# Relative-position softmax: 32 partitions of one late store move to an indirect transfer on GpSimd's queue

## The chip, the cores and the metric

One core of a Trainium2 chip runs the kernel. The metric is the device time of one execution in microseconds (us); less is better. Three executions of the kernel before took 1331.39 to 1331.63 us, median 1331.4.

## What is computed

The reference adds a bias to a stack of 2 x 8 square float32 matrices of S = 2112 rows and columns, and takes a softmax over each row. The bias depends on the head and on the distance of row and column alone, clipped to 16 on either side:

```
rel = pos[:, None] - pos[None, :]
rel_clipped = np.clip(rel, -16, 16) + 16
bias = rel_bias[:, rel_clipped]
logits = logits + bias[None, :, :, :]
logits = logits - logits.max(axis=-1, keepdims=True)
exp = np.exp(logits)
return exp / exp.sum(axis=-1, keepdims=True)
```

Input and output have 285 MB each. Nothing is used twice, so each byte is loaded once and stored once.

## The kernel before

**Tiling.** The 2 x 8 x 2112 rows are dealt to the 128 partitions in blocks: each partition owns 264 rows that follow one another (`ROWS`). The work goes in 44 chunks (`N`), numbered 0 to 43 here; a chunk is six rows (`R`) of every partition, that is 128 pieces of 6 x 2112 x 4 = 50,688 bytes, each in one piece in memory. Four buffers `X0` to `X3` (`NBUF`) hold four chunks; chunk n lies in buffer n mod 4. Chunks 40 to 43 are the last four, and chunk 41, "the last but two", lies in `X1`.

**Staging.** SyncE (SP) issues all loads (line 89) and all stores (line 93) on its queue, q1. VectorE (DVE) adds the bias to a row and takes its negated maximum in one instruction (line 181), ScalarE (ACT) takes the exponential and the row sum (line 190), VectorE takes the reciprocal (line 198) and scales (line 202). All of it works in place in the buffer. The bias comes out of a strip `F` that VectorE copies from `M` in PSUM once for 24 rows (line 175); `M` is built at the start from `rel_bias` and two iotas that GpSimd (POOL) writes (lines 112 and 113).

**What sets the order.** The order is written out by hand; there is no scheduler. `take(engine, semaphore, n)` (line 84) waits until a semaphore has n and takes n off it again. VectorE raises `scaled` once per scaled row. SyncE's stream is:

- six loads of one row each and three of a chunk, for chunks 0 to 3 (lines 98 to 103);
- the store of five rows of chunk 0 (line 219), and its sixth row in 17 transfers (lines 221 to 232), the "fan". The list `FAN` (lines 42 to 47) splits the partitions into nine lanes of every ninth partition, and each lane into two transfers, of k and of the remaining partitions; sorted, they have 15, 14, 13, 12, 11, 10, 9, 8, 7, 7, 6, 5, 4, 3, 2, 1 and 1 rows;
- a loop over chunks (lines 233 to 237): wait for six scaled rows of chunk n, store it, wait until the store of chunk n - 1 has landed (semaphore `st` of its buffer), load chunk n + 3 into that buffer;
- behind the loop, the stores of chunks 41 and 42 (line 239) and the two halves of chunk 43 (lines 240 and 241), which raise `landed`; then waits for the stores still under way (line 243), and for `landed` (line 244).

Load 43 is the last load. It is issued before store 41 and stands ahead of it in the queue.

**GpSimd** writes the two iotas, and at lines 114 to 117 waits for the store of line 219 and the fan, and raises `st[0]` in place of the store of chunk 0. Then it has nothing to do until the end.

Of the kernel before, what the change touches and what calls it, by code (L numbers as in the profile page):

```python
# [8 lines left out]
I32 = mybir.dt.int32  # L9
EXP = mybir.ActivationFunctionType.Exp  # L10
ALU = mybir.AluOpType
# [4 lines left out]
def kernel(  # L16
# [6 lines left out]
    nc = tc.nc  # L23
    P = 128
    B, H, S, S2 = logits.shape
# [3 lines left out]
    ROWS = B * H * S // P  # L29
    PB = S // ROWS  # L30
    assert ROWS * P == B * H * S and PB * ROWS == S and PB == H == 8
    R = 6
    NBUF = 4
    STEP = R * NBUF
    N = ROWS // R
# [2 lines left out]
    MW = S + ROWS - 1  # L38
    FW = S + STEP - 1
    BIG = 3.0e38  # L40
    LANES = 9
    FAN = []
    for lane in range(LANES):
        m = len(range(lane, P, LANES))
        k = 15 if lane == 0 else 15 - lane
# [4 lines left out]
    io = ctx.enter_context(tc.tile_pool(name="io", bufs=1))  # L50
    X = [io.tile([P, R * S], FP32, tag=f"X{b}", name=f"X{b}") for b in range(NBUF)]
# [2 lines left out]
    nmax = io.tile([P, STEP], FP32, tag="nmax", name="nmax")  # L54
    tot = io.tile([P, STEP], FP32, tag="tot", name="tot")
    rec = io.tile([P, STEP], FP32, tag="rec", name="rec")
    ip = io.tile([P, 3, PB], I32, tag="ip", name="ip")
    ps = ctx.enter_context(tc.tile_pool(name="ps", bufs=1, space=bass.MemoryType.PSUM))
    M = ps.tile([P, 4096], FP32, tag="M", name="M")

    def view(t, offset, dims):

        return bass.AP(tensor=t.tensor, offset=t.offset + offset, ap=[[list(t.ap[0])[0], P]] + dims)

    def rows(t, j, n):

        return bass.AP(tensor=t.tensor, offset=t.offset + j * S, ap=[[ROWS * S, P], [1, n * S]])

    with tc.tile_critical(no_gpsimd_drain=True):
        ld = [nc.alloc_semaphore(f"ld{b}") for b in range(NBUF)]  # L70
        st = [nc.alloc_semaphore(f"st{b}") for b in range(NBUF)]
        added = nc.alloc_semaphore("added")
        expd = nc.alloc_semaphore("expd")
        scaled = nc.alloc_semaphore("scaled")
# [2 lines left out]
        pre = nc.alloc_semaphore("pre")  # L77
        idx = nc.alloc_semaphore("idx")
        dve = nc.alloc_semaphore("dve")
        main = nc.alloc_semaphore("main")  # L80
        fan = [nc.alloc_semaphore(f"fan{i}") for i in range(2)]
        landed = tc.alloc_semaphore("landed")

        def take(eng, sem, n):
            eng.wait_ge(sem, n).then_inc(sem, -n)  # L85


        def load(j, b):
            nc.sync.dma_start(out=X[b][:, :], in_=rows(logits, j, R)).then_inc(ld[b], 16)

        def store(j, b, s0=0, n=R, sem=None):
            take(nc.sync, scaled, n)
            nc.sync.dma_start(
                out=rows(out, j + s0, n), in_=X[b][:, s0 * S : (s0 + n) * S]
            ).then_inc(sem or st[b], 16)


        for r in range(R):
            nc.sync.dma_start(
                out=X[0][:, r * S : (r + 1) * S], in_=rows(logits, r, 1)  # L100
            ).then_inc(ld[0] if r == R - 1 else pre, 16)
        for n in range(1, NBUF):
# [6 lines left out]
            out=rbB,  # L109
            in_=bass.AP(tensor=rel_bias.tensor, offset=rel_bias.offset, ap=[[0, P], [1, H * W]]),  # L110
        ).then_inc(rb, 16)
        nc.gpsimd.iota(ip[:, 0], pattern=[[0, PB]], base=0, channel_multiplier=1).then_inc(idx, 1)
        nc.gpsimd.iota(ip[:, 2], pattern=[[1, PB]], base=0, channel_multiplier=0).then_inc(idx, 1)  # L113
        take(nc.gpsimd, main, 16)
        take(nc.gpsimd, fan[0], 16 * ((len(FAN) + 1) // 2))
        take(nc.gpsimd, fan[1], 16 * (len(FAN) // 2))
        nc.gpsimd.sem_inc(st[0], 16)

        v = nc.vector
        done = [0]  # L120
# [21 lines left out]
        for m, op in ((eq, ALU.is_equal), (gt, ALU.is_gt), (le, ALU.is_le), (lt, ALU.is_lt)):  # L142
# [4 lines left out]
            out=view(F, 0, [[W, H], [1, W]]), in0=view(F, 0, [[W, H], [1, W]]),  # L147
# [3 lines left out]
                             axis=mybir.AxisListType.X, op=ALU.add))  # L151
# [5 lines left out]
            out=view(F, 0, [[W, PB], [1, W]]), in0=view(F, SC + 2 * PB, [[1, PB], [0, W]]),  # L157
# [7 lines left out]
            out=view(M, U, [[ROWS, PB], [1, W]]), in0=view(F, 0, [[W, PB], [1, W]]),  # L165
            in1=view(F, SC + 8 * PB, [[1, PB], [0, W]]), op=ALU.add))
        then(v.tensor_copy(out=view(M, U + W, [[ROWS, PB], [1, ROWS - W]]),  # L167
                           in_=view(F, SC + 7 * PB, [[1, PB], [0, ROWS - W]])))
# [8 lines left out]
        def add(b):  # L177
            take(v, ld[b], 16)
            for r in range(b * R, (b + 1) * R):
                x = X[b][:, (r - b * R) * S : (r - b * R + 1) * S]  # L180
                v.tensor_tensor_reduce(  # L181
                    out=x, in0=x, in1=F[:, STEP - 1 - r : STEP - 1 - r + S], scale=-1.0, scalar=BIG,
                    op0=ALU.add, op1=ALU.min, accum_out=nmax[:, r : r + 1],
# [37 lines left out]
        for i, (k, g, lane) in enumerate(FAN):  # L221
            p = g * LANES + lane
            nc.sync.dma_start(
                out=bass.AP(
                    tensor=out.tensor, offset=out.offset + (p * ROWS + R - 1) * S,
                    ap=[[LANES * ROWS * S, k], [1, S]],
                ),
                in_=bass.AP(
                    tensor=X[0].tensor, offset=X[0].offset + p * PSX + (R - 1) * S,
                    ap=[[LANES * PSX, k], [1, S]],  # L230
                ),
            ).then_inc(fan[i % 2], 16)
        with nc.Fori(0, ROWS - 2 * STEP + 1, STEP, engines=[ENG.SP]) as j:
            for b in range(NBUF):
                store(j + (b + 1) * R, (b + 1) % NBUF)
                take(nc.sync, st[b], 16)
                load(j + (b + NBUF) * R, b)
        for n in range(N - NBUF + 1, N - 1):
            store(n * R, n % NBUF)
        store((N - 1) * R, (N - 1) % NBUF, 0, HALF, landed)  # L240
        store((N - 1) * R, (N - 1) % NBUF, HALF, R - HALF, landed)
        for b in range(NBUF - 1):
            take(nc.sync, st[(N + b) % NBUF], 16)
    nc.sync.wait_ge(landed, nc.sync.to_reg(32), synchronizes=[nc.sync.lower_ap(out)])


# [28 lines left out]
```

## Time and profile before

| What | us |
|---|---|
| median of three executions | 1331.4 |
| the profiled execution | 1331.3 |
| span of that execution, from its first to its last instruction | 1329.5 |
| VectorE busy | 976.7 |
| ScalarE busy | 575.2 |
| GpSimd busy | 0.4 |
| share of the span on queue q1, as a share of 16 DMA engines | 99.5% |
| DMA rate over the span | 430 GB/s |

The profile is one execution. Its times are microseconds from the first instruction; `L93` is line 93 of the kernel. `SPq` is the part of SyncE that issues DMAs. A "DMA issue" row gives the size of a transfer and the time from its issue to its landing. A row for a window gives the busy time of each engine in that stretch, then the granted clock of TensorE (not used here), the mean busy share of the 16 DMA engines, and GB/s. A transfer counts in the window in which it starts, so short windows can read over 1.

### The profile page before, as it was taken

Reading aid. Unit: us, or ns where it says so; the run is one execution under the profiler, and the core shown is the slowest. Engines: PE = TensorE matmul, PEld = TensorE weight load, DVE = VectorE, ACT = ScalarE, POOL = GpSimd, SP = SyncE. Lnnn points to the kernel's source line nnn. Section 1 sums busy time; section 2 is a strip of 40 time slices with the busy share of each in tenths; the row PEclk is TensorE's granted clock in tenths of the full one; section 3 lists DMA queues with packets and bytes.
Section 4 is the critical chain, followed back from the end, with each engine's and each line's share of the span. In section 5 each row is a group of like instructions: output and inputs, shape, how many; then the busy total and the mean of one; then the engine's idle time right before and its main releaser. Section 6 shows DMA issues by size and latency. Waiting matters only on the chain. (4 is left out here: it accounts for less than half of the span.)

```text
span 1329.5 us, 2477 instructions
## 1 busy us (share of the span) xinstructions
DVE 976.7 (73%) x911; ACT 575.2 (43%) x539; POOL 0.4 (0%) x6
## 2 busy tenths in 40 slices
DVE  5998767777877776787778767677877776687772
ACT  2565333444444343345444333444444343345440
POOL 0000000000000000000000000000000000000000
DMA  9999999999999999999999999999999999999997
GB/s 391 427 426 424 436 430 433 438 433 435 432 435 435 433 436 430 436 433 435 430 433 439 433 433 427 439 435 432 433 432 438 430 433 430 436 430 436 438 432 337
DMA packets 13939, 571.12 MB, mean 430 GB/s; under 512 B 1648, under 2 KB 1776, under 8 KB 1776
## 3 DMA queue, kind: packets, MB, share of 16 engines
q1 hardware_dynamic: 13792, 570.96, 99.5%
q10 hardware_dynamic: 144, 0.14, 0.1%
q14 instruction: 3, 0.02, 0.0%
HBM read 285.61 MB, written 285.47 MB: 430 GB/s over the span
## 5 line engine op out<-in xcount | busy, mean ns | idle before, releaser
L181 DVE CUSTOM_DVE_ANT_0 X<-X,F 128x2112 f32<-128x2112 f32 x264 | 605.2, 2354 | 302.0 <-DVEq L85 302.0
L190 ACT ACTIVATE X<-X,nmax 128x2112 f32<-128x2112 f32 x264 | 541.7, 2052 | 538.2 <-ACTq L85 516.4
L202 DVE TENSOR_SCALAR X<-X,rec 128x2112 f32<-128x2112 f32 x264 | 332.5, 1316 | 13.2
L190 ACT ACT_TABLE_LOAD x11 | 14.1, 1283 | 185.8 <-ACTq L85 185.8
L190 ACT ACTIVATION_READ_ACCUMULATOR X<-X,nmax 128x1 f32 x264 | 49.2, 186 | 0.0
L175 DVE COPY F<-M 128x2135 f32 x11 | 26.1, 2375 | 6.6 <-DVEq L85 6.6
L181 DVE DVE_READ_ACCUMULATOR2_ANT nmax<- 128x1 f32 x264 | 21.7, 82 | 0.0
L198 DVE RECIPROCAL rec<-tot 128x3 f32<-128x3 f32 x88 | 15.0, 170 | 0.0
L146 DVE TENSOR_TENSOR F<-F 128x264 f32<-128x264 f32 x1 | 0.4, 435 | 4.9 <-DMA F<-in_rel_bias_dram 4.9
L167 DVE COPY M<-F 128x1848 f32<-128x1848 f32 x1 | 2.1, 2077 | 0.0
L133 DVE TENSOR_SCALAR ip<-ip 128x8 int32<-128x8 int32 x1 | 0.2, 172 | 1.3 <-POOL ip L113 1.3
L150 DVE TENSOR_REDUCE rbS<-F 128x33 f32<-128x264 f32 x1 | 0.6, 610 | 0.0
L164 DVE TENSOR_TENSOR M<-F 128x264 f32<-128x264 f32 x1 | 0.4, 441 | 0.0
L156 DVE TENSOR_TENSOR F<-F,rbS 128x264 f32<-128x264 f32 x1 | 0.4, 426 | 0.0
L143 DVE TENSOR_SCALAR F<-F 128x8 f32<-128x8 f32 x4 | 0.4, 167 | 0.0
L169 DVE COPY M<-rbS 128x247 f32<-128x247 f32 x1 | 0.4, 406 | 0.0
L154 DVE TENSOR_SCALAR F<-F,rbS 128x8 f32<-128x8 f32 x1 | 0.2, 231 | 0.0
L160 DVE SCALAR_TENSOR_TENSOR F<-F,rbS 128x8 f32<-128x8 f32 x1 | 0.2, 227 | 0.0
L155 DVE TENSOR_SCALAR F<-F,rbS 128x8 f32<-128x8 f32 x1 | 0.2, 225 | 0.0
L161 DVE SCALAR_TENSOR_TENSOR F<-F,rbS 128x8 f32<-128x8 f32 x1 | 0.2, 221 | 0.0
L136 DVE TENSOR_TENSOR F<-ip 128x8 f32<-128x8 int32 x1 | 0.2, 167 | 0.0
L139 DVE TENSOR_TENSOR F<-ip 128x8 f32<-128x8 int32 x1 | 0.2, 167 | 0.0
(9 smaller groups left out, 1.2 us busy)
## 6 DMA issues: line engine op xcount, KB each, us to landing
X<-in_logits_dram SPq DMA_DIRECT2D x43, 6336.0 KB, 44.7
out_dram<-X SPq DMA_DIRECT2D x42, 6336.0 KB, 52.8
X<-in_logits_dram SPq DMA_DIRECT2D x6, 1056.0 KB, 12.6
out_dram<-X SPq DMA_DIRECT2D x2, 3168.0 KB, 21.9
out_dram<-X SPq DMA_DIRECT2D x1, 5280.0 KB, 34.9
F<-in_rel_bias_dram ACTq DMA_DIRECT2D x1, 132.0 KB, 6.4
out_dram<-X SPq DMA_DIRECT2D x1, 123.8 KB
out_dram<-X SPq DMA_DIRECT2D x1, 115.5 KB
```

The source lines that it names most:

```text
L143: then(v.tensor_scalar(out=m, in0=dp, scalar1=0.0, scalar2=None, op0=op))
L146: then(v.tensor_tensor(out=view(F, 0, [[W, H], [1, W]]), in0=view(F, 0, [[W, H], [1, W]]), in1=view(F, SC + 3 * PB, [[1, H], [0, W]]), op= ...
L150: then(v.tensor_reduce(out=rbS[:, :], in_=view(F, 0, [[1, W], [W, H]]), axis=mybir.AxisListType.X, op=ALU.add))
L156: then(v.tensor_tensor(out=view(F, 0, [[W, PB], [1, W]]), in0=view(F, SC + 2 * PB, [[1, PB], [0, W]]), in1=view(rbS, W - 1, [[0, PB], [-1, ...
L164: then(v.tensor_tensor(out=view(M, U, [[ROWS, PB], [1, W]]), in0=view(F, 0, [[W, PB], [1, W]]), in1=view(F, SC + 8 * PB, [[1, PB], [0, W]] ...
L167: then(v.tensor_copy(out=view(M, U + W, [[ROWS, PB], [1, ROWS - W]]), in_=view(F, SC + 7 * PB, [[1, PB], [0, ROWS - W]])))
L169: then(v.tensor_copy(out=M[:, 0:U], in_=low.to_broadcast([P, U])))
L175: v.tensor_copy(out=F[:, :], in_=M[:, bass.ds(ROWS - STEP - j, FW)]).then_inc(dve, 1)
L181: v.tensor_tensor_reduce(out=x, in0=x, in1=F[:, STEP - 1 - r : STEP - 1 - r + S], scale=-1.0, scalar=BIG, op0=ALU.add, op1=ALU.min, accum_ ...
L190: nc.scalar.activation(out=x, in_=x, func=EXP, scale=-1.0, bias=nmax[:, r : r + 1], accum_out=tot[:, r : r + 1],).then_inc(expd, 1)
L198: v.reciprocal(out=rec[:, r0 : r0 + HALF], in_=tot[:, r0 : r0 + HALF]).then_inc(inv, 1)
L202: v.tensor_scalar_mul(out=x, in0=x, scalar1=rec[:, r : r + 1]).then_inc(scaled, 1)
```

## The change

The store of chunk 41 is split by partition. SyncE stores partitions 0 to 95 as before, with one transfer of 96 pieces. Partitions 96 to 127 (`OWN` to `P`) are stored by GpSimd with indirect transfers: the output is seen as 5632 blocks of 12,672 numbers, one per partition and chunk, and a column of the new tile `sel` has, for each source partition of a transfer, the number of the block that it goes to. `PLAN` lists the transfers as (partitions n, first partition p0, range a to b of the partitions really stored). Partitions outside a to b get a block number past the end (`FAR`), and the transfer skips such pieces (`bounds_check`, `oob_is_err=False`). There are two entries: (112, 0, 0, 0) names partitions 0 to 111 and skips all; (48, 80, 96, 128) names 80 to 127, skips the first 16 and stores the other 32.

GpSimd makes the two columns at the start, an iota and two selects each. After its old waits it waits for `ready`, which SyncE raises once it has seen the six scaled rows of chunk 41, and issues the two transfers. At the end SyncE waits for both (`soft`) beside `landed`. The computation is the same.

```diff
+    OWN = 96
+    PLAN = [(112, 0, 0, 0), (48, 80, OWN, P)]
+    FAR = 1 << 20
+    sel = io.tile([P, len(PLAN)], I32, tag="sel", name="sel")
...
+        for w, (n, p0, a, b) in enumerate(PLAN):
+            col = sel[:, w : w + 1]
+            step(g.iota(col, pattern=[[0, 1]], base=p0 * N + N - 3, channel_multiplier=N))
+            for base, mul in ((p0 - a, 1), (b - 1 - p0, -1)):
+                g.wait_ge(pool, made[0])
+                step(g.affine_select(out=col, in_=col, pattern=[[0, 1]], base=base, channel_multiplier=mul,
+                                     compare_op=ALU.is_ge, fill=float(FAR)))
+        take(g, pool, made[0])
...
+        take(g, ready, 1)
+        blocks = out.rearrange("b h s t -> (b h s t)").rearrange("(n c) -> n c", c=R * S)
+        late = X[(N - 3) % NBUF]
+        lap = list(late.ap[0])[0]
+        for w, (n, p0, a, b) in enumerate(PLAN):
+            g.indirect_dma_start(
+                out=blocks, out_offset=bass.IndirectOffsetOnAxis(ap=sel[0:n, w : w + 1], axis=0),
+                in_=bass.AP(tensor=late.tensor, offset=late.offset + p0 * lap, ap=[[lap, n], [1, R * S]]),
+                in_offset=None, bounds_check=P * N - 1, oob_is_err=False,
+            ).then_inc(soft, 16)
...
-        for n in range(N - NBUF + 1, N - 1):
-            store(n * R, n % NBUF)
+        take(nc.sync, scaled, R)
+        nc.sync.sem_inc(ready, 1)
+        nc.sync.dma_start(
+            out=bass.AP(
+                tensor=out.tensor, offset=out.offset + (N - 3) * R * S, ap=[[ROWS * S, OWN], [1, R * S]]
+            ),
+            in_=X[(N - 3) % NBUF][0:OWN, :],
+        ).then_inc(st[(N - 3) % NBUF], 16)
+        store((N - 2) * R, (N - 2) % NBUF)
...
+    nc.sync.wait_ge(soft, nc.sync.to_reg(16 * len(PLAN)), synchronizes=[nc.sync.lower_ap(out)])
```

More of the change, by code (lines that the diff above doesn't have):

```diff
@@ L40 @@
     BIG = 3.0e38
+    OWN = 96
+    PLAN = [(112, 0, 0, 0), (48, 80, OWN, P)]
+    FAR = 1 << 20
+    assert sorted(p for n, p0, a, b in PLAN for p in range(a, b)) == list(range(OWN, P))
     LANES = 9
@@ L79 @@
         dve = nc.alloc_semaphore("dve")
+        ready = nc.alloc_semaphore("ready")
+        pool = nc.alloc_semaphore("pool")
+        soft = tc.alloc_semaphore("soft")
         main = nc.alloc_semaphore("main")
@@ L113, with step @@
         nc.gpsimd.iota(ip[:, 2], pattern=[[1, PB]], base=0, channel_multiplier=0).then_inc(idx, 1)
+        g = nc.gpsimd
+        made = [0]
+        def step(ins):
+            made[0] += 1
+            ins.then_inc(pool, 1)
+        for w, (n, p0, a, b) in enumerate(PLAN):
[6 more added lines that the diff above has]
+        take(g, pool, made[0])
         take(nc.gpsimd, main, 16)
```

## The prediction

> **What bounds the kernel now.** I read the page first: its totals, then the DMA lines.
>
> ```profile
> span 1329.5 us, 2477 instructions
> DVE 976.7 (73%) x911; ACT 575.2 (43%) x539; POOL 0.4 (0%) x6
> DMA  9999999999999999999999999999999999999997
> DMA packets 13939, 571.12 MB, mean 430 GB/s; under 512 B 1648, under 2 KB 1776, under 8 KB 1776
> q1 hardware_dynamic: 13792, 570.96, 99.5%
> ```
>
> No compute engine is full; the 16 DMA engines are, in 39 slices of 40, and nearly all their work is one queue, q1, SyncE's. 430 GB/s over 16 engines is 26.9 GB/s each, so one row of a chunk (50,688 bytes) costs an engine 1.89 us, a whole chunk (128 rows, 8 per engine) 15.1 us, and one single row of S (8,448 bytes) 0.31 us. The mean of 430 holds short idle at both ends, so these prices are high by a per cent or so. The chain of waits ends in the last scale on VectorE, at 1304.9 us, and says nothing of the 24 us behind it; SyncE's own waits do (the row below it):
>
> ```profile
> 1302.33 2.54 DVE X L202 x2
> ...
> SPq L244 <- DMA out_dram<-X: 14.6, 1, 14.6
> ```
>
> The last thing waited for is the landing of the last store. Now the end of the schedule, from SyncE's timeline and the DMA issues of short windows (load 43, then the stores of chunks 41, 42, and the two halves of 43):
>
> ```profile
> X<-in_logits_dram SPq DMA_DIRECT2D x1, 6336.0 KB, 44.8
> ...
> 1244.93 60.38 SPq L93 DMA_DIRECT2D out_dram<-X  x4
> ...
> out_dram<-X SPq DMA_DIRECT2D x1, 6336.0 KB, 53.0
> ...
> out_dram<-X SPq DMA_DIRECT2D x1, 6336.0 KB, 38.6
> ...
> out_dram<-X SPq DMA_DIRECT2D x1, 3168.0 KB, 20.1
> ...
> out_dram<-X SPq DMA_DIRECT2D x1, 3168.0 KB, 23.6
> ```
>
> and when the four were issued and when load 43 was:
>
> ```profile
> 1238.15 0.35 SPq L89 DMA_DIRECT2D X<-in_logits_dram  x1
> ...
> 1274.95 30.36 SPq L93 DMA_DIRECT2D out_dram<-X  x3
> ...
> 1300.97 0.33 SPq L93 DMA_DIRECT2D out_dram<-X  x1
> ...
> 1304.97 0.33 SPq L93 DMA_DIRECT2D out_dram<-X  x1
> ```
>
> Load 43 lands at 1282.95, store 41 at 1297.9, store 42 at 1313.55, the halves of 43 at 1321.1 and 1328.6. The spaces of 15 and twice 7.5 us are the price of a chunk and of a half: on the engine that lands last, every transfer starts as the one before it ends, and its time is rows times 1.89 us. The other engines are seen in the tail, microsecond by microsecond (third figure from the right: granted clock; then DMA share, GB/s):
>
> ```profile
> 1320.00:1321.00 1.00, 0.00 (x0) 0.00 (x0) 0.00 (x0) 1.00 0.77 329
> 1321.00:1322.00 1.00, 0.00 (x0) 0.00 (x0) 0.00 (x0) 1.00 0.59 253
> 1322.00:1323.00 1.00, 0.00 (x0) 0.00 (x0) 0.00 (x0) 1.00 0.41 177
> 1323.00:1324.00 1.00, 0.00 (x0) 0.00 (x0) 0.00 (x0) 1.00 0.41 177
> 1324.00:1325.00 1.00, 0.00 (x0) 0.00 (x0) 0.00 (x0) 1.00 0.24 101
> 1325.00:1326.00 1.00, 0.00 (x0) 0.00 (x0) 0.00 (x0) 1.00 0.18 76
> 1326.00:1327.00 1.00, 0.00 (x0) 0.00 (x0) 0.00 (x0) 1.00 0.06 25
> 1327.00:1328.00 1.00, 0.00 (x0) 0.00 (x0) 0.00 (x0) 1.00 0.06 25
> ```
>
> A share of 0.06 is one engine of 16. About nine are done by 1322 to 1323, seven still run until 1324, four into 1325, and one alone ends near 1328.1. The shares from 1320 on sum to 2.7 us, so equal loads would end all engines near 1322.7: **5.4 us (0.4%) is the most that moving rows between engines can bring.** Why unequal? In the first chunk, line 223 stores one row per partition by 17 transfers of 15, 14, 13 ... 1, 1 rows. If a transfer of k rows takes the same first k engines, the first engine gets 17 such rows and the last none: 17 times 0.31 is a skew of 5.3 us, near the 7 us seen. Then the six engines with 11 to 17 rows are late by the code, and the tail's seven are these six and one more.
>
> **The change part by part.** The program order on each engine is from the two listings; only POOL, and SyncE at the store of chunk 41, differ.
>
> Start: POOL gets two more iotas and four selects. The nearest rows are its iotas, and the tail of the run gives POOL's and SyncE's small instructions:
>
> ```profile
> 1.04 0.13 POOL L112 IOTA ip<- 128x8 int32 x1 [0.59 <-PEq L270]
> 1.13 0.14 POOL L113 IOTA ip<- 128x8 int32 x1
> ...
> L270 SPq EVENT_SEMAPHORE  x2: 17/17/17, 1329.0 to 1329.5; - x2
> L270 POOLq EVENT_SEMAPHORE_RANGE_CLEAR  x1: 71/71/71, 1329.2 to 1329.2; - x1
> ```
>
> Six times 0.14 is 0.8 us at 1.3 us; they come behind the two iotas that VectorE waits for, and are wanted at 1245. Nothing, unless they took a thousand times as long.
>
> SyncE: the wait for six scaled rows is the old one; the semaphore raise is 0.02 us; the store of 96 rows is issued like that of 128 (0.34). Behind it stand the issues at 1274.95 and later: 30 us of cover. At the end SyncE also waits for the two indirect transfers, begun 80 us before: nothing.
>
> POOL's new wait for that raise has nothing behind it but the two indirect issues and the closing barrier. No row shows an indirect issue; the nearest are 0.33 us for SyncE's. Bounded by zero and ten times that for each: the rows enter the DMA engines between 1246 and 1252. They go by another queue, so they need not stand behind load 43 as store 41 does; they are taken in among load 42, store 40 and load 43. POOL's program has one more instruction behind the last barrier: 0.1 us, on the path (range 0 to 0.5).
>
> DMA work: store 41 gives each engine six rows in place of eight: minus two rows, 3.77 us, on all. The 32 rows come back somewhere. No view shows an indirect transfer, so their division is bounded by cases: even (two each, nothing changes) and in blocks. In blocks, 48 rows over 16 engines are three consecutive ones each; the 16 skipped ones are those of engines 0 to 4 and one of engine 5, so 0 to 4 get none, 5 gets two, 6 to 15 three. I take **blocks**: only they give a meaning to a window of 48 whose first 16 are skipped; for an even spread 32 rows would do. The sum by engine then is minus 3.77 us on 0 to 4, nothing on 5, plus 1.89 on 6 to 15.
>
> [...]
>
> Applied to the tail: the last engine, at 1328.1, is one of the loaded ones and goes to 1324.4; engine 5 stays somewhere between 1324 and 1326; the nine early ones go from at most 1322.5 to 1324.4. The seventh late engine is not among the first six, so it gets one row more: from the near edge of the three that end in 1324 to 1325, 1324.1, to **1326.0. It ends the kernel**, 2.1 us sooner than now. The far edges: it is not late in other runs (minus 3.7 us), or it ends now at 1326.2 (then 1328.1, no gain).
>
> What must not slip: the rows taken in ahead delay load 43 on the engines that get three, by 5.66 us. The seventh engine is 4.0 us ahead of the last, so load 43 lands some 1.7 us later, and so do the scales and the last two issues: 1302.7 and 1306.7. Data follow an issue by about 1.4 us (loads issued at 0.96 us; the DMA share is 0.01 until 2 us and 0.76 from 2 to 4):
>
> ```profile
> 0.96 3.27 SPq L99 DMA_DIRECT2D X<-in_logits_dram  x6
> ...
> 0.00:2.00 2.00, 0.63 (x5) 0.00 (x0) 0.42 (x6) 1.00 0.01 3
> 2.00:4.00 2.00, 0.43 (x5) 0.00 (x0) 0.00 (x0) 1.00 0.76 158
> ```
>
> So the first half is ready at 1304.1. The earliest engine reaches it at 1320.9 less two halves, 1305.8 (now), 1307.7 with its extra row; a relieved one at 1324.6 less 15.1 less 3.77, 1305.7. Covered by 1.6 us; were load 43 late by the whole 5.66 us, the relieved engines would stand idle for 2.3 us. Chunk 42 has more cover, VectorE idle before its next add:
>
> ```profile
> 1283.08 2.36 DVE L181 CUSTOM_DVE_ANT_0 X<-X,F 128x2112 f32<-128x2112 f32 x1 [8.22 <-DVEq L85]
> ```
>
> Sum: the profiled execution took 1331.3 us (span 1329.5 and 1.8 around it), the median is 1331.4. Minus 2.1, plus 0.1, from the median: **1329.4 us.** Its own range is 1327.7 (3.7 gained) to 1331.5 (nothing).
>
> **The rivals.** (1) *The 96 rows take as long as 128.* If the rate of a store depends on which partitions it reads, the lower engines stay at eight row times, the relief is lost and the upper ones still get three rows. Middle engines that end at 1322.4 then end at 1328.1, the seventh at up to 1329.8: 1331.4 to 1333.1. Against it: 17 unequal transfers of line 223 leave no hole in the DMA share; nothing else in the trace has fewer than 128 partitions. [...]
>
> (2) *Even spread.* Two rows each: the ends stay, load 43 is 3.77 us late on the last engine, the first half is ready at 1306.2, 0.4 us late for early engines alone. 1331.5. It would also be the result if the change did not do what its window says.
>
> (3) *Skipped rows are not free*, the slower one. 112 and 16 skipped rows are eight per engine. If each takes time on its engine as a moved row does, that is 15.1 us more on every engine, between 1246 and 1270, and load 43 and all behind it end later: 1344.5. A cost of nothing is what the word skip says; no row decides. It outweighs the gain of 2.1 us from 0.26 us per row, and passes 0.2% from 0.6 us (8 times 0.6 less 2.1 is 2.7); at a third of a row's price it gives 1334.4.
>
> **How the numbers follow.** Two tenths of a per cent, 2.7 us, is about what a measurement of this kernel can tell from no change: 1328.7 and 1334.1. Blocks with free skips: 0.55, of which 0.30 below 1328.7 (the seventh engine's lag may differ in the runs that are timed, and the last engine alone would give 3.7) and 0.25 within. Rival 1: 0.13, of it 0.10 within and 0.03 slower. Rival 2: 0.10, 0.07 and 0.03 (if it meets rival 1 the lower engines carry 3.77 us more, 1335.2). Rival 3: 0.15, slower. 0.07 for what an indirect transfer costs beyond all this, slower. Faster 0.30, same 0.42, slower 0.28. The range goes from 1327.7 to 1335.2, the end of rival 2 with 1; above it lie most of rival 3 and of the rest.
>
> **What would show it.** In the tail of the DMA share after the change: blocks right, if it falls from near 1 to nothing within some 3 us in place of 7, about 1323 to 1326; rival 1, if the share dips between 1283 and 1298, in store 41; rival 2, if the tail is as now; rival 3, if the packets or bytes of GpSimd's queue count more than 32 rows (1.62 MB), or load 43's add starts 10 us late. The step on load 43 is right if that add starts at 1284 to 1286. I am wrong at the root if the last engine now is not one of those with many rows in the first chunk.

## The result and the profile after

The kernel after takes 1335.53 us, the median of eight executions (1334.43 to 1338.07), the kernel before 1331.43 (1331.31 to 1331.72). The ratio is 1.0032, 95% interval 1.0021 to 1.0043: **4.1 us slower**, where 2.0 us faster was forecast. The profiled execution took 1335.25 us. Its page first:

```profile
span 1333.5 us, 2498 instructions
DMA packets 14099, 571.12 MB, mean 428 GB/s; under 512 B 1808, under 2 KB 1936, under 8 KB 1936
q1 hardware_dynamic: 13760, 569.33, 99.2%
q0 software_dynamic: 192, 1.62, 0.3%
```

The bytes are those of before. 1.62 MB, 32 rows, went to GpSimd's queue q0, and 160 packets of hardly any bytes with them: one for each of the 128 skipped rows, and 16 more for each of the two transfers (with one transfer of 48 rows, in no112, q0 has 64 packets). Queue q1 is as full as it was, and yet the span is 4.0 us longer. SyncE's last transfers, from the DMA issues of short windows (KB, then us from issue to landing; load 43 and the stores of chunks 41, 42 and the halves of 43):

```profile
X<-in_logits_dram SPq DMA_DIRECT2D x1, 6336.0 KB, 46.7
...
out_dram<-X SPq DMA_DIRECT2D x1, 4752.0 KB, 57.0
...
out_dram<-X SPq DMA_DIRECT2D x1, 6336.0 KB, 42.0
...
out_dram<-X SPq DMA_DIRECT2D x1, 3168.0 KB, 20.7
...
out_dram<-X SPq DMA_DIRECT2D x1, 3168.0 KB, 24.8
```

With the issues at 1238.45, 1245.32, 1275.29, 1303.18 and 1307.57 they land at 1285.15, 1302.3, 1317.3, 1323.9 and 1332.4. Load 43 is 2.2 us later than before; then store 41, a quarter smaller than it was, lands 4.4 us later than it did, and the transfers behind it land 2.8 to 3.8 us later. VectorE's add of chunk 43 shows the first part, the wait in brackets:

```profile
1285.29 2.36 DVE L214 CUSTOM_DVE_ANT_0 X<-X,F 128x2112 f32<-128x2112 f32 x1 [10.12 <-DVEq L93]
```

The second part is in the windows in which store 41 runs (DMA share, then GB/s, last). The kernel before:

```profile
1285.00:1290.00 5.00, 5.00 (x7) 4.30 (x4) 0.00 (x0) 1.00 0.96 416
1290.00:1295.00 5.00, 5.00 (x6) 4.61 (x5) 0.00 (x0) 1.00 1.05 456
1295.00:1300.00 5.00, 4.85 (x6) 3.98 (x4) 0.00 (x0) 1.00 1.01 436
```

The kernel after:

```profile
1285.00:1290.00 5.00, 4.71 (x5) 2.15 (x2) 0.00 (x0) 1.00 1.02 355
1290.00:1295.00 5.00, 5.00 (x5) 4.68 (x5) 0.00 (x0) 1.00 0.99 314
1295.00:1300.00 5.00, 4.85 (x6) 4.74 (x5) 0.00 (x0) 1.00 0.97 355
```

This pair is the finding. The engines are as busy as before, but move less: the share is near 1 and the rate falls by 15, 31 and 19%. The "busy" engines with a falling rate are here engines whose packets take longer, not engines with more to do: of the rows begun between 1276 and 1304 the slowest took 4.31 us, where before none took more than 1.90. The missing 284 GB/s (1308 less 1024) over 5 us are 1.42 MB, or 3.3 us of all 16 engines at 430 GB/s. The tail then has the old shape, later:

```profile
1322.00:1323.00 1.00, 0.00 (x0) 0.00 (x0) 0.00 (x0) 1.00 0.94 406
1323.00:1324.00 1.00, 0.00 (x0) 0.00 (x0) 0.00 (x0) 1.00 0.82 355
...
1325.00:1326.00 1.00, 0.00 (x0) 0.00 (x0) 0.00 (x0) 1.00 0.59 253
...
1328.00:1329.00 1.00, 0.00 (x0) 0.00 (x0) 0.00 (x0) 1.00 0.29 127
...
1331.00:1332.00 1.00, 0.00 (x0) 0.00 (x0) 0.00 (x0) 1.00 0.06 25
```

The shares of the twelve microseconds from 1320 to 1332 sum to 6.5 us, so equal loads would end near 1326.5, 3.8 us later than before, and the last engine still ends some 5.5 us behind that mean. Not even the spread of the ends was narrowed.

Two more sources are used below, which no view shows. The trace's packet records have the start, the length and the size of each packet, but name no engine. Chained by their ends (in the kernels before and after, all but some 70 of 14,000 packets start within 12 ns of the end of another) they fall into 16 sequences, each taken here as one engine; figures from that are marked *chained*, and where several engines run in step two sequences can be swapped. The trace also has 16 *landing events* for each whole transfer, taken here as one for each engine; they need no chaining.

### The profile page after: what moved, and what is told of

The parts are those of the page before. It is cut to its first block, busy times and chain, and to the rows that moved or that the text cites. A ratio compares the mean times of both kernels' runs of the same rounds, so it can differ in the third digit from the quotient of the medians.

```text
span 1333.5 us, 2498 instructions
## 1 busy us (share of the span) xinstructions
DVE 976.7 (73%) x911; ACT 575.2 (43%) x539; POOL 3.3 (0%) x14
## 3 DMA queue, kind: packets, MB, share of 16 engines
q0 software_dynamic: 192, 1.62, 0.3%
## 5 line engine op out<-in xcount | busy, mean ns | idle before, releaser
L223 ACT ACT_TABLE_LOAD x11 | 14.1, 1283 | 185.8 <-ACTq L93 185.8
```

Of the source, the lines that this page charges most:

```text
L223: nc.scalar.activation(out=x, in_=x, func=EXP, scale=-1.0, bias=nmax[:, r : r + 1], accum_out=tot[:, r : r + 1],).then_inc(expd, 1)
```

## The experiments

Two theories stood against each other. **R**: the rate of a store depends on which partitions its engines read at the same time, and falls with 96 of the 128; such a fall is called a crowd below. **E**: the number of rows on each engine is all that counts, and the loss comes from the indirect transfer; in experiment 5, where that had fallen, E is that a store of fewer than 128 partitions is slow as such. Beside them stood the skipped rows, and the question where a gain could be had.

**1. The machinery without moved rows (skip).** Both indirect transfers are issued with all rows skipped; SyncE stores all 128.

```diff
-    OWN = 96
-    PLAN = [(112, 0, 0, 0), (48, 80, OWN, P)]
+    OWN = P
+    PLAN = [(112, 0, 0, 0), (48, 80, 0, 0)]
```

> The changed kernel with both indirect transfers skipping all their rows, and the store of chunk 41 whole, 128 partitions, on SyncE's queue: the machinery alone. Theories R and E: 1331.4 to 1331.8, no dip in the rate. Theory S (skipped rows or the software queue cost the engines time): some of the 4.1 us, 1332.5 to 1336.

```profile
q0 software_dynamic: 192, 0.00, 0.0%
```

1331.52 us (1331.27 to 1331.89), ratio 1.0001 (0.9992 to 1.0011): no change. 160 skipped rows, two issues, the columns, the raise and the added wait cost nothing that can be measured. In the kernel after the issues have these rows in GpSimd's timeline, 1.07 and 0.88 us, three times SyncE's 0.33:

```profile
1246.25 1.07 POOL L146 DMA_INDIRECT out_dram<-X,sel  x1 [1243.44 <-POOLq L93]
1247.63 0.88 POOL L146 DMA_INDIRECT out_dram<-X,sel  x1 [0.30 <-issue]
```

**2. The store of 96 rows alone (low96).** The kernel before, with store 41 cut to partitions 0 to 95; the other 32 rows are left out, and GpSimd does nothing.

```diff
-        for n in range(N - NBUF + 1, N - 1):
-            store(n * R, n % NBUF)
+        take(nc.sync, scaled, R)
+        nc.sync.dma_start(... ap=[[ROWS * S, 96], [1, R * S]] ..., in_=X[(N - 3) % NBUF][0:96, :])
+        store((N - 2) * R, (N - 2) % NBUF)
```

> The kernel before, with the store of chunk 41 cut to partitions 0 to 95 on SyncE's queue; the other 32 partitions of that chunk are left out of the output, and GpSimd does nothing new. Theory R (the rate of a store falls where its rows lie on few partitions): the DMA rate dips between 1283 and 1300 to about 315 to 355 GB/s at a full busy share, as in the changed kernel, although no indirect transfer runs; the two engine-rows saved are mostly eaten, and the time is 1329.5 to 1333. Theory E (only the number of rows per engine counts): no dip, every engine ends 3.77 us sooner, 1327.6.

1337.76 us (1337.67 to 1337.87), ratio 1.0047 (1.0030 to 1.0064): **1.6 MB less is moved, and it takes 6.3 us more.** Its windows:

```profile
1280.00:1285.00 5.00, 2.06 (x1) 0.00 (x0) 0.00 (x0) 1.00 1.10 365
1285.00:1290.00 5.00, 5.00 (x7) 4.30 (x5) 0.00 (x0) 1.00 1.07 365
1290.00:1295.00 5.00, 5.00 (x5) 4.74 (x5) 0.00 (x0) 1.00 0.85 264
1295.00:1300.00 5.00, 4.85 (x6) 3.85 (x4) 0.00 (x0) 1.00 0.96 375
```

The dip is there without any indirect transfer. E is out. R held as to the dip, but the time that it gave, 1329.5 to 1333, was too low. By the landing events, five engines land store 41 11.2 us behind load 43, six times 1.87. The other eleven, 1.3 to 6.1 us behind these five at load 43, are 3.5 to 16.7 us behind them at store 41.

The cut store alone is also 2.2 us slower than the kernel after, which moves 1.6 MB more. The price is not a fixed one: in sum, the rows begun between 1276 and 1304 take 72 us longer than 1.87 us each here and 55 us in the kernel after (0.1 in the kernel before).

**3. The same bytes from all partitions (thin128).** Store 41 takes the first three quarters of each of the 128 pieces; the rest is left out. The diff is against low96.

```diff
-                ap=[[ROWS * S, 96], [1, R * S]],
-            in_=X[(N - 3) % NBUF][0:96, :],
+                ap=[[ROWS * S, 128], [1, R * S * 3 // 4]],
+            in_=X[(N - 3) % NBUF][0:128, 0 : R * S * 3 // 4],
```

> The kernel before, with chunk 41 stored from all 128 partitions on SyncE's queue but only the first three quarters of each partition's 50,688 bytes: as many bytes as in low96, and the last quarter is left out of the output. Theory R (which partitions a store reads decides): no dip in the DMA rate; all engines end 3.7 us sooner, 1327.7, which is 10 us below low96. Theory B (a store of fewer bytes, or the landing of chunk 41 sooner, is what disturbs the end): a dip as in low96, 1333 or more.

1327.75 us (1327.48 to 1328.07), ratio 0.9972 (0.9962 to 0.9983), and no dip in the same windows:

```profile
1285.00:1290.00 5.00, 5.00 (x7) 4.27 (x4) 0.00 (x0) 1.00 1.00 433
1290.00:1295.00 5.00, 5.00 (x7) 4.60 (x6) 0.00 (x0) 1.00 1.09 471
```

This is the relief of 3.77 us that the prediction counted on. It exists, 10.0 us below low96 for the same bytes; so it isn't the smaller store, or its earlier landing, that disturbs the end.

**4. The upper 96 (up96), and the lower 96 to other places in memory (cross96).** up96 stores partitions 32 to 127 and leaves 0 to 31 out; cross96 reads partitions 0 to 95 and writes them where 32 to 127 belong.

```diff
 up96:    offset ... (32 * ROWS + (N - 3) * R) * S, in_=X[(N - 3) % NBUF][32:128, :]
 cross96: offset ... (32 * ROWS + (N - 3) * R) * S, in_=X[(N - 3) % NBUF][0:96, 0 : R * S]
```

> As low96, but partitions 32 to 127 of chunk 41 are stored and 0 to 31 left out. Theory R: the partitions that crowd are now the upper 64, whose rows are moved by the engines that are early; the late, lowest-numbered engines carry the lower partitions and save their two rows. A dip in the rate as in low96, but a time of 1327.6 to 1330, and 1.5 us or more below low96. Theory E: the same as low96, 1327.6, no dip.

> As low96, from partitions 0 to 95 on chip, but written to the places in memory that belong to partitions 32 to 127; the output is then wrong for chunk 41 (the lowest 32 partitions' places stay empty). Theory R with the source on chip as its cause: as low96, 1337 to 1338.5. Theory H (the places in memory crowd): as up96, 1328.9 to 1330.4.

cross96 takes 1337.78 us (1337.16 to 1338.25), the same as low96: the places in memory don't matter, the source on the chip does. up96 takes 1329.59 (1328.93 to 1330.35), ratio 0.9985 (0.9975 to 0.9995). Its dip is nearly that of low96:

```profile
1285.00:1290.00 5.00, 5.00 (x5) 4.21 (x4) 0.00 (x0) 1.00 1.14 355
1290.00:1295.00 5.00, 5.00 (x7) 4.61 (x6) 0.00 (x0) 1.00 0.90 304
```

In sum its rows take 63 us longer than 1.87 us each, where those of low96 take 72 and those of cross96 74. So most of the 8 us between the two is not in the total but in who pays. Chained: in low96 the engine that is last anyway stretches its six rows by 10.7 us and ends at 1334.7, from 1328.1 less 3.8; in up96 it has no stretch there, and those that stretch by 7 us were early ones.

**5. Half the rows, packed or spread (low64, comb64).** Store 41 has 64 rows, of partitions 0 to 63, or of every second partition; the other 64 are left out. Four rows for each engine in both.

```diff
 low64:  ap=[[ROWS * S, 64], [1, R * S]],      in_: partitions 0 to 63
 comb64: ap=[[2 * ROWS * S, 64], [1, R * S]],  in_: ap=[[2 * PSX, 64], [1, R * S]]
```

> Store 41 has the 64 rows of partitions 0 to 63; the other 64 are left out and nothing goes by GpSimd. The same number of rows on each engine, and the same bytes, as in the store of every second partition run beside it. R: the rate falls to some 300 GB/s or less while store 41 runs and the engines stretch; the four rows take nearly as long as eight and the next store is held up too: 1329 to 1336. E: 1323.9, as the other.

> Store 41 has 64 rows, of every second partition (0, 2, ... 126); the other 64 are left out and nothing goes by GpSimd. Each engine gets four rows in place of eight, and they lie on all of the chip's partitions. R (the partitions read at the same time set the rate, not the number of rows): no dip of the rate, all engines 7.5 us sooner, 1331.4 - 7.5 = 1323.9, with up to 1.5 us lost if engines reach the halves of chunk 43 before they are ready: 1323.5 to 1325.5. E (a store of fewer than 128 partitions is slow as such): as slow as the store of 64 low partitions run beside it.

comb64: 1324.19 us (1323.95 to 1324.28), as forecast. low64: 1327.17 (1326.28 to 1328.65), below the range given, but 3.0 us above comb64. Windows of low64, then of comb64:

```profile
1280.00:1285.00 5.00, 1.21 (x1) 0.00 (x0) 0.00 (x0) 1.00 1.02 264
1285.00:1290.00 5.00, 5.00 (x5) 3.59 (x3) 0.00 (x0) 1.00 0.93 233
```

```profile
1285.00:1290.00 5.00, 5.00 (x5) 3.86 (x3) 0.00 (x0) 1.00 0.98 426
...
1295.00:1300.00 5.00, 4.85 (x7) 4.29 (x4) 0.00 (x0) 1.00 0.73 314
```

With partitions 0 to 63 the rate at a full share falls to 250 to 260 GB/s, under two thirds; with every second partition it doesn't fall. (comb64's 314 at 1295 is the other kind of low rate: the share is low too, 0.73, and 0.63 from 1300 to 1305; the first half of chunk 43 is issued in 1301 to 1303, the second in 1304 to 1308, and from 1305 the share is 1.13.) The number of rows in a store isn't the cause; which partitions they are read from is. low64 came out lower than forecast since the crowd costs less than a halved rate: chained, an engine's four rows and what follows them are stretched by 2.9 to 6.3 us, not by 7.5.

Put to a full share, the windows of low96 (experiment 2) give 332, 341 and 311 GB/s (365 over a share of 1.10, 365 over 1.07 and 264 over 0.85), and there the landing events have five engines unslowed and eleven slowed; those of low64 give 259 and 250, with neighbouring transfers in the windows. Why these partitions slow each other, no run here shows.

**6. Without the skipped 112 (no112), and with it twice (twoskip).** The same 32 rows are moved; only the wholly skipped transfer ahead of them changes.

```diff
 no112:   PLAN = [(48, 80, OWN, P)]
 twoskip: PLAN = [(112, 0, 0, 0), (112, 0, 0, 0), (48, 80, OWN, P)]
```

> The changed kernel without the wholly skipped transfer of 112; its 32 rows go by the transfer of 48 alone. Theories R and E: the rows enter the engines some 13 us sooner, at about 1250 in place of 1265; the time stays at 1334.4 to 1338. Theory S: below 1333.5.

> The kernel after with the wholly skipped transfer of 112 rows issued twice. If each skipped row takes one turn between two rows of SyncE's queue (14 turns of 1.87 us on each engine), the 32 real rows enter some 13 us later, at 1278 to 1290, behind load 43 and among the rows of store 41; the add of chunk 43 on VectorE then starts at 1282.5 to 1283.5 in place of 1285.3. The time: the collision in store 41 stays, and 32 more rows of other partitions are read beside it: 1334 to 1338. If a skipped row is only dropped at once: the same as after in all, the add at 1285.3.

Queue q0 (packets, MB, share) in the windows 1246 to 1262 and 1262 to 1280, of the kernel after:

```profile
q0 software_dynamic: 101, 0.00, 0.4%
...
q0 software_dynamic: 91, 1.62, 21.0%
```

In the first 16 us only packets without bytes go, and all 32 rows follow behind 1262. Without the 112, the same two windows:

```profile
q0 software_dynamic: 50, 1.47, 30.5%
...
q0 software_dynamic: 14, 0.15, 2.4%
```

With the 112 twice, 1262 to 1280 and 1280 to 1296:

```profile
q0 software_dynamic: 173, 0.56, 10.5%
...
q0 software_dynamic: 43, 1.06, 18.4%
```

So a skipped row costs its engine next to no time (each of these packets takes 9 ns in the kernel after; skip has a ratio of 1.0001), but takes a turn: the engine goes back to SyncE's queue for a row after each. Chained, in 140 of the 176 steps from one packet of q0 to the next on an engine of the kernel after, just one row of 50,688 bytes of SyncE's stands between. The 101 packets are six per engine in the 13 us from the second issue, one in 2.1 us, near the 1.89 us of a row. **The skipped 112 are a delay line**: seven turns on each engine, some 13 us (the first packet of q0 starts at 1251.2, the first of the 32 rows at 1265.0). They decide beside which transfer the 32 rows are read: store 40 (no112), load 43 (after), store 41 in large part (twoskip). The times are 1340.26 us (1337.40 to 1343.05), ratio 1.0068 (1.0049 to 1.0087); 1335.53; and 1341.88 (1337.72 to 1347.11), ratio 1.0090 (1.0064 to 1.0117). Beside a store the rows crowd its readers; beside a load they hardly do here, and after is the best of the three. The rows begun between 1246 and 1262 take 31 us longer in sum than 1.87 us each in no112, and 1.2 us in after; those begun between 1262 and 1276, most of them beside load 43, take 6.5 us longer in after. Two windows while the rows of no112 go beside store 40, of the kernel before and then of no112 (395 over a share of 1.17 is 338, 335 over 0.82 is 409):

```profile
1255.00:1260.00 5.00, 5.00 (x7) 4.30 (x4) 0.00 (x0) 1.00 0.98 426
1260.00:1265.00 5.00, 5.00 (x5) 4.62 (x5) 0.00 (x0) 1.00 1.05 456
```

```profile
1255.00:1260.00 5.00, 5.00 (x5) 4.15 (x4) 0.00 (x0) 1.00 1.17 395
1260.00:1265.00 5.00, 5.00 (x7) 4.61 (x7) 0.00 (x0) 1.00 0.82 335
```

Load 43 lands with what is read ahead of it. The add of chunk 43 in no112, and in twoskip:

```profile
1290.01 2.36 DVE L214 CUSTOM_DVE_ANT_0 X<-X,F 128x2112 f32<-128x2112 f32 x1 [14.99 <-DVEq L93]
```

```profile
1283.15 2.36 DVE L214 CUSTOM_DVE_ANT_0 X<-X,F 128x2112 f32<-128x2112 f32 x1 [8.35 <-DVEq L93]
```

In twoskip the load is back where it was before (1283.08), and the time is 6 us above after all the same: the delay of load 43 is not what made the kernel slow. (The profiled execution of twoskip was the fastest of its four, 1337.72, so the trace shows 2 of these 6 us.) In no112 the load is 4.7 us later than in after, and its share of the loss isn't separated from that of store 40. Both times lie above the ranges given, so the price of rows beside a store was again set too low.

**7. The fan taken out (nofan).** Chunk 0 is stored whole by one transfer of 128; the 17 transfers go, and GpSimd's waits for them.

```diff
-        nc.sync.dma_start(out=rows(out, 0, R - 1), in_=X[0][:, 0 : (R - 1) * S]).then_inc(main, 16)
-        for i, (k, g, lane) in enumerate(FAN):
...
+        nc.sync.dma_start(out=rows(out, 0, R), in_=X[0][:, :]).then_inc(main, 16)
```

> The kernel before without the 17 unequal transfers: the sixth row of chunk 0 is stored together with the other five by one transfer of 128 partitions. If the lowest-numbered engines are late because of those transfers, they end 0.9 to 2.8 us sooner, and the last engine, with 12 of those rows in place of 8, ends 1.3 us sooner: 1330.1. If they are not the cause: 1331.4.

1330.61 us (1329.41 to 1332.99), ratio 0.9994 (0.9985 to 1.0003): nothing that can be told. Its tail still has four to five engines late:

```profile
1322.00:1323.00 1.00, 0.00 (x0) 0.00 (x0) 0.00 (x0) 1.00 0.29 127
...
1325.00:1326.00 1.00, 0.00 (x0) 0.00 (x0) 0.00 (x0) 1.00 0.24 101
1326.00:1327.00 1.00, 0.00 (x0) 0.00 (x0) 0.00 (x0) 1.00 0.12 51
```

Unequal ends come from the fan only in part. By the landing events, the last engine lands load 4 (at 110 us) 4.2 us behind the first in the kernel before and 1.9 us behind in nofan, so the fan does make a skew; but in nofan five engines then fall back step by step, to between 4.5 and 7.0 us at the end, and the other eleven stay within 1.9. Those are slow-downs over the whole run, and what makes them stays open.

**8. The relief without the crowd (spread, spread2).** SyncE stores five of the six rows of S of all 128 partitions, and the sixth of partitions 0 to 5; GpSimd stores the other sixths, 8,448 bytes each, dealt so that the engines late before get fewer.

```diff
 spread:  PLAN = [(112, 0, 0, 0), (128, 0, 48, P), (48, 0, 16, 48), (16, 0, 6, 16)]
 spread2: PLAN = [(112, 0, 0, 0), (128, 0, 56, P), (48, 16, 48, 56), (48, 0, 16, 48), (16, 0, 6, 16)]
```

> The changed kernel's idea without cutting the partitions: SyncE stores five of the six rows of chunk 41 from all 128 partitions; of the sixth row, partitions 0 to 5 go on SyncE's queue (8,448 bytes each) and the rest by indirect transfers of 8,448-byte pieces, in windows (128, from partition 48), (48, 16 to 47) and (16, 6 to 15) behind the same skipped 112, which lie on engines 6 to 15 but for two pieces on engine 5. By blocks: engines 0 to 4 lose 2.2 us, 6 to 15 gain 1.25. Theory R: no large dip, since the main store stays whole, and an end at about 1326.0 in place of 1328.1: 1329.2, from 1328.5 to 1330.5. If the small pieces crowd as the large ones did: 1331 or more.

> The whole output, with all partitions in each large transfer: SyncE stores five of the six rows of chunk 41 for all partitions, and for partitions 0 to 5 the sixth; GpSimd stores the sixth of the others by indirect transfers that leave engines 0 to 4 with fewer pieces, the last engine (4) among them. Each of engines 0 to 4 does 7 pieces of 0.31 us less, 2.2 us; the others take 3 or 4 more, about 1.1 us, which they have to spare. R: 1331.4 - 2.2 = 1329.2, range 1328.5 to 1330.2, no dip of the rate. If the lateness of the last engine in other runs than the profiled one does not come from the same engines, it gives less: 1330 to 1331.4.

spread: 1330.88 us (1330.58 to 1331.52), ratio 0.9996 (0.9987 to 1.0005). spread2: 1331.28 (1330.87 to 1331.64), 0.9999 (0.9989 to 1.0008). Both are over 4 us better than after, and neither is better than before by more than can be measured; the 1329.2 that R gave for both was missed. Chained, in spread the window of 128 isn't dealt in blocks of eight: two engines move eight of GpSimd's 122 pieces and one moves six, where blocks of eight would give ten engines twelve each and one two, and the engine that ends last got four of its pieces back, 1.26 us. The counts fit a deal by four partitions at a time; that is an estimate from them, since the records name no partition. spread2 takes partitions 48 to 55 out of that window and mends it. The tail of spread2:

```profile
1323.00:1324.00 1.00, 0.00 (x0) 0.00 (x0) 0.00 (x0) 1.00 0.24 101
1324.00:1325.00 1.00, 0.00 (x0) 0.00 (x0) 0.00 (x0) 1.00 0.06 25
...
1326.00:1327.00 1.00, 0.00 (x0) 0.00 (x0) 0.00 (x0) 1.00 0.06 25
```

Fifteen engines now end by about 1324, which is what the change was built to do; one goes on into the microsecond from 1326. Chained, it ends at 1327.5, 0.6 us sooner than before in place of 2.2, and it is the engine that was last before. By the landing events it lands load 43 0.2 us later than before, and its part of store 41, which is 2.5 us shorter, only 1.2 us sooner: some 1.1 us is lost there, while GpSimd's pieces are read. Why that engine is late in both kernels isn't settled.

## Why the prediction was wrong

The measured 1335.53 us lies above the whole range, 1327.7 to 1335.2. That it is near the upper end is chance: the end stood for an even spread of the 32 rows together with rival 1, and the spread is not even. Step by step:

- **What bounds the kernel: right.** Equal loads, 5.4 us of skew at most, and a last engine with many rows in the first chunk (chained, 12 of them). That a transfer of k rows takes the same first k engines was an assumption, which no run shows; that the fan makes the skew was only partly right (nofan).
- **Start, SyncE, GpSimd, closing: right.** Two issues took 2.0 us where 0 to 6.6 was allowed, and skip shows the sum of all to be nothing that can be measured.
- **The division in blocks: right.** Chained, five engines get none of the 32 rows, one two and ten three.
- **The entry "between 1246 and 1252": wrong.** The rows go behind 1262, after the turns of the skipped ones. This cost nothing and by luck spared 5 us (no112): nothing in the prediction counted on it.
- **Load 43: right.** The add was forecast 1.7 us later, within 1284 to 1286; it came 2.2 us later, at 1285.29. twoskip shows that it isn't the cause.
- **"Store 41 gives each engine six rows in place of eight: minus two rows, 3.77 us, on all": this step failed.** Rows were priced by the mean rate, whatever partitions they came from. Six rows from all partitions do save it (thin128, minus 3.7 us); six rows from partitions 0 to 95 cost 6.3 us (low96). Chained, the 11 lower engines of the kernel after lost 3.7 us in store 41 on the mean, just the relief, but between 1.6 and 8.2 us each, and the other five lost none. (The sum, 41 us, comes out of the landing events too.)
- **That the seventh engine ends the kernel at 1326.0: fell with it.** The last, at 1332.0, is an engine that was early. The sum closes: 1320.9 before, minus two rows and plus three, 1.9, plus 8.2 of stretch, is 1331.0; the rest, 1 us, is put down to rows slowed in other transfers, beside load 43 among them.
- **Rival 1 was the right one and priced too low.** It gave the lower engines eight row times each, the author's estimate, hence 1331.4 to 1333.1. No run shows eight on each: in the kernel after eight was the mean of eleven engines; the worst took ten (six times 1.89 and 8.2 make 19.5 us), and it was one with three indirect rows. Its sign, written as a dip of the share between 1283 and 1298, came as a dip of the rate at a full share. The argument against it, no hole in the DMA *share* during the fan, was worth nothing, since a crowded engine keeps its share and loses its *rate* (0.99 and 314 GB/s).
- **Rivals 2 and 3 are out**: the division is not even, and skipped rows are free in engine time (skip: 160 of them, ratio 1.0001).

## What to carry to other kernels

Price a store by the partitions that are read at the same time, not by its bytes: cut work off a store by taking bytes from all partitions (thin128, 3.7 us less), not by dropping partitions at one end (low96, 6.3 us more for the same bytes). Look for a crowd in the rate at a full share (314 GB/s at 0.99 in the kernel after), since the share alone doesn't show it. Where a queue is balanced to a few microseconds, an average price per row decides nothing; what counts is what the last engine gets (low96 and up96 lose 72 and 63 us in sum, and their times are 8.2 us apart).

## What was not expected of the hardware

- A skipped row of an indirect transfer stands in the packet records as a packet of 4 bytes, and takes one turn against the other queue: 101 of them in some 13 us on 16 engines while SyncE's rows of 50,688 bytes go between. Here an engine changed queues after one such row (chained, in 140 of 176 steps of the kernel after).
- The page's line of bytes written counts skipped rows as if they were written, though the packets don't have them:

```profile
HBM read 285.61 MB, written 293.58 MB: 436 GB/s over the span
```

  That is skip; before has 285.47, and 160 rows of 50,688 bytes are the 8.11 MB between.
- Reading rows of one store beside another store cost far more here than beside a load. Over the six windows of 5 us from 1245 to 1275 the rates of before sum to 2606, of after to 2556 and of no112 to 2373: 0.6 us of all engines lost by after, 2.7 by no112 (the difference times 5 us, over 430).
